# Seven more weights in the one-operand form, and one norm chain in place of two, in a two-block layer of GEMMs on one core

## The chip, the cores and the metric

The kernel runs on one core of a Trainium2 chip: TensorE (PE, the matmuls), VectorE (DVE), ScalarE (ACT), GpSimd (POOL) and SyncE (SP, which issues most transfers). Each engine works through its own instructions in the order in which they were written to it. The metric is the device time of one execution in microseconds, as the median of several runs; less is better.

## The reference

Two blocks work on one sequence of 256 tokens with 2048 features, all in fp32:

```python
# first block
h  = rms_norm(x); u = h @ w_in
y  = concat(ssd_mixer(u[...]), rwkv7_mixer(u[...]))
x1 = x + y @ w_out                                  # w_outa, w_outb
x1 = x1 + memory_cross_attention(rms_norm(x1), mem, wq, wk, wv, wo)
f  = square(relu(rms_norm(x1) @ w1)) @ w2           # w2 as w2a, w2b, w2c
o  = rms_norm(x1 + f, final_norm_g)
# second block
h  = rms_norm(o, attn_norm_g); u = h @ w_in2 + b_in
a  = sliding_window_attention(q, k, v, sinks)       # q, k, v from u
s  = s5_ssm(...)                                    # a diagonal complex recurrence, then gelu and a GLU
x2 = x1 + merge(gates from u, a @ w_ba, s @ w_bs) @ w_out2
x2 = x2 + conv_gated_ffn(rms_norm(x2))              # w_up, w_da, w_db
y  = rms_norm(x2, end_norm_g)
```

The two norms at the seam matter here. With p3 the sum of squares of x over the features and p4 that of x times the final norm's weight, the first is 1/sqrt(p3/D + eps) = c3, the second 1/sqrt(c3^2 p4/D + eps) = c4, and the input of w_in2 is x with both weights times c3 c4.

## The kernel before

Activations lie transposed, 128 features by 256 tokens, and each is kept as hi and lo, two tiles whose sum is the fp32 value. Weights are streamed in units of 128x1024 numbers. For each unit the core gets a transfer (raw), an ACT cast to hi (`wh`) and a DVE subtraction that leaves lo (`wl`). Then TensorE sums wh·hi + wh·lo + wl·hi in PSUM for each K-tile of 128x128 weights. In the narrow form these are three matmuls of 256 columns. In the wide form, which the table `WIDE` (line 29) gives to the first so many blocks of a weight, hi and lo lie side by side and are one operand of 512 columns:

```python
if pair and wide:
    both = acts[c + k].rearrange("p a n -> p (a n)")
    ops = ((pss[n], wh[:, k, s], both), (o, wl[:, k, s], hi))
else:
    ops = ((o, wh[:, k, s], hi), (o, wh[:, k, s], lo), (o, wl[:, k, s], hi))
```

The wide form leaves its sum in two halves of a PSUM bank. At the end of an output's K-tiles, `gemm` folds them: an ACT copy of the second half into a tile `fold...` from the pool `tm` (8 tiles, shared with the rotation tables of the SSM), and a DVE add of the first half. In the narrow form the evacuation reads PSUM itself. Matmuls rotate through 4, 5 or 7 PSUM banks (`NMM, NMB, NMC`), by phase; the second projection runs with five.

Beside the GEMMs run side chains as Python generators (the cross attention, the sliding window attention with its softmax, `ws`, `wsc`, `wp`, `wt`, `wo`, the SSM `s5`, the norms), stepped by a meter that keeps an estimate of each engine's time (tables `FIXED` and `RATE`). A scheduler then sets the order of each engine's instructions from its own estimate of when each could start, so the order on an engine is not that of the code. `s5` works in pairs of channel tiles: `bu` (matmuls), a rotation by the tables `tc` and `tsn` (the tiles r1, r2), a scan (`xi`), the rotation back, `py` (matmuls), gelu. Each of its tables is six GpSimd products of 128x256 in `s5_table` (line 1281). `norm34` (line 1656) makes the two norms at the seam, c3 with `rms_col`, then c4 with `rsqrt_small`, which takes fifteen or so DVE instructions on 128x2 numbers each; `row` turns the result into a row that every evacuation of w_in2 multiplies by (`evac_in2`, line 1684).

In the trace w_in2 goes by the name `w_in` (a number at the end of a name is left out), w1 by `w`, and w_out2, w_outa by `w_out`, `w_outa`. All operations are recorded by one helper, hence L268 throughout.

Of the kernel before, what the change touches and what calls it, by code (L numbers as in the profile page):

```python
# [14 lines left out]
ALU = mybir.AluOpType  # L15
# [3 lines left out]
D = 2048  # L19
EPS = 1e-6  # L20
# [5 lines left out]

NMM, NMB, NMC = 4, 5, 7

WIDE = {"w_in": 8, "w1": 16, "w2a": 4, "w2b": 4, "w2c": 2, "w_out2": 4, "w_up": 22, "w_da": 4, "w_db": 4}


LIVE, OL, LAT, XS = 4, 4, 0.28, 1.0
# [25 lines left out]
def _flat(w, widths):  # L58
# [3 lines left out]
    for width in widths:  # L62
# [7 lines left out]
CUT_D = [512] * 3 + [256, 128, 128]  # L70
# [2 lines left out]
CUT_O = [256] * 8  # L73
SEQ = [("w_in", range(len(CUT_IN))), ("wk", range(len(CUT_K))), ("wv", range(4)), ("w_outa", range(len(CUT_O))), ("w_outb", range(len(CUT_O))), ("wq", range(4)), ("wo", range(4)),
       ("w1", range(6)), ("w2a", range(4)), ("w1", range(6, 11)), ("w2b", range(4)),
       ("w1", range(11, 16)), ("w2c", range(4)), ("w_in2", range(12)), ("w_ba", range(4)),
       ("w_glu", range(2)), ("w_bs", range(4)), ("w_out2", range(4)), ("w_up", range(11)), ("w_da", range(4)),
       ("w_up", range(11, 22)), ("w_db", range(len(CUT_D)))]
WIDTHS = {
    "w_in": CUT_IN,  # L80
    "wk": CUT_K, "wv": [512] * 4, "w_outa": CUT_O, "w_outb": CUT_O, "wq": [512] * 4, "wo": [512] * 4,
    "w1": [512] * 16, "w2a": [512] * 4, "w2b": [512] * 4, "w2c": [512] * 4,
    "w_in2": [512] * 11 + [256],
    "w_glu": [512] * 2, "w_ba": [512] * 4, "w_bs": [512] * 4, "w_out2": [512] * 4,
    "w_up": [512] * 22, "w_da": [512] * 4, "w_db": CUT_D,
# [218 lines left out]
class Net:  # L304
# [54 lines left out]
    def pair(self, pl, name, dt=F32):  # L359
        return pl.tile([P, 2, S], dt, tag="p", name=name)  # L360
# [123 lines left out]
    def gemm(self, name, acts, evac, blocks=None, moving_w=False, hook=None):  # L484
# [5 lines left out]
        for blk in (range(len(widths)) if blocks is None else blocks):  # L490
            width = widths[blk]
            wide = blk < WIDE.get(name, 0)
            base = sum(widths[:blk]) // P
# [787 lines left out]
    def s5_table(self, i):  # L1281

        gp = self.nc.gpsimd
        (cl, sl), (ch, sh) = self.tab
        lo = lambda a: a[:, i].unsqueeze(1).broadcast_to((P, 16, 16))
        hi = lambda a: a[:, i].unsqueeze(2).broadcast_to((P, 16, 16))
        w = lambda a: a.rearrange("p (a b) -> p a b", a=16)
        tmp = lambda n: self.tm(f"{n}{i}")
        c, s, t = self.g(f"tc{i}"), self.g(f"tsn{i}"), tmp("tt")
        self.mul(w(c), hi(ch), lo(cl), gp)  # L1290
        self.mul(w(t), hi(sh), lo(sl), gp)
        self.sub(c, c, t, gp)
        t = tmp("tu")
        self.mul(w(s), hi(sh), lo(cl), gp)
        self.mul(w(t), hi(ch), lo(sl), gp)
        self.add(s, s, t, gp)
        return c, s

    def s5(self):
        nc = self.nc  # L1300
        nxt = self.s5_table(0)
        b2 = lambda a: a.broadcast_to((P, 2, S))
        pair = lambda a: a.rearrange("p (a t) -> p a t", a=2)
        for qd in range(4):
            uh, ul = self.split(self.u2[qd], f"u2s{qd}")
            bh, bl = self.s5b
            y = self.t(f"s5y{qd}")
            for e0 in (0, 2):
                rot = []
                pts = self.pst2(f"bu{4 * qd + e0}")  # L1310
                rows = [slice(32 * e, 32 * e + 32) for e in (e0, e0 + 1)]
                self.beside([(pts[d][:, a * S:(a + 1) * S], b[rows[d], a, qd], u[rows[d]], n == 0, n == 2)
                             for a in range(2) for n, (b, u) in enumerate(((bl, uh), (bh, ul), (bh, uh))) for d in range(2)])
                i0 = 4 * qd + e0
                tabs, turned = [], []
                for d in range(2):
                    w = pair(pts[d])
                    ct, sn = (a.unsqueeze(1) for a in nxt)
                    nxt = self.s5_table(i0 + d + 1) if i0 + d < 15 else None
                    t1, t2 = pair(self.t2(f"r1_{i0 + d}")), pair(self.t2(f"r2_{i0 + d}"))  # L1320
                    self.mul(t1, w, b2(ct))
                    self.mul(t2, w, b2(sn))
                    tabs.append((ct, sn))
                    turned.append((t1, t2))
                yield
                for d in range(2):
                    i = i0 + d
                    (ct, sn), (t1, t2) = tabs[d], turned[d]
                    self.add(t1[:, 0], t1[:, 0], t2[:, 1])
                    self.sub(t1[:, 1], t1[:, 1], t2[:, 0])  # L1330
                    xi = pair(self.t2(f"xi_{i}"))
                    mg = self.s5mag[:, i:i + 1].broadcast_to((P, S))
                    for a in range(2):
                        nc.vector.tensor_tensor_scan(xi[:, a], mg, t1[:, a], 0.0, op0=ALU.mult, op1=ALU.add)
                    self.mul(t1, xi, b2(ct))
                    self.mul(t2, xi, b2(sn))
                    self.sub(t1[:, 0], t1[:, 0], t2[:, 1])
                    self.add(t1[:, 1], t1[:, 1], t2[:, 0])
                    rot.append(t1)
                    yield  # L1340
                py = self.pst(f"py{qd}{e0}")
                self.beside([(py[32 * e:32 * e + 32, :S], cz[:, 4 * qd + e], rot[e - e0][:, a], a == 1, a == 0)
                             for a, cz in ((1, self.czi), (0, self.czr)) for e in (e0 + 1, e0)])
                r = slice(32 * e0, 32 * e0 + 64)
                self.stt(y[r], self.u2[qd][r], self.v("ssm_d", qd)[r], py[r, :S], ALU.mult, ALU.add)
                yield
            self.act(y, y, AF.Gelu)
            self.gl[qd] = self.split(y, f"gl{qd}")
            yield
# [3 lines left out]
def tile_net(ctx, tc, io, out):  # L1353
    m = Net(ctx, tc, io)
    nc = m.nc
    pool = lambda name, bufs: ctx.enter_context(tc.tile_pool(name=name, bufs=bufs))
# [9 lines left out]
    R, C = m.R, m.C  # L1366
# [217 lines left out]
    m.gemm("w_outb", Late(mix, 8), evac_o1)  # L1584
    mix = m.mix = None
    m.banks(NMB, "b")
    m.side(m.norm_rows(acc1, D, EPS, "x"))
    m.qT, m.oT = [None] * 16, [None] * 16

# [42 lines left out]
    xb, acc3, acc4 = [None] * 16, m.g("acc3"), m.g("acc4")  # L1632
# [23 lines left out]
    def norm34():  # L1656
        yield
        yield
        c3 = m.rms_col(acc3, D, EPS, "r3")
        p4 = m.col_sums(acc4, "r4ss")  # L1660
        v4 = m.small("r4v", 2)
        m.mul(v4, c3, c3)
        m.mul(v4, v4, p4[:, 0:2])
        m.ts(v4, v4, 1.0 / D, EPS, ALU.mult, ALU.add)
        c4 = m.rsqrt_small(v4, 2, "r4")
        c34 = m.small("c34", 2)
        m.mul(c34, c3, c4)
        yield
        R["r34"] = m.row(c34, "row34")
        yield  # L1670
        R["r3"] = m.row(c3, "row3")

    m.side(norm34())
    bq8 = m.sp.tile([P, 8], F32, tag="bq8", name="bq8", bufs=1)
    late(m.ts(bq8, m.v("b_q", 0, 8), 0.125, None, ALU.mult))
# [149 lines left out]
```

## Time and profile before

| | |
|---|---|
| median of three runs (lowest, highest) | 2894.16 us (2894.05, 2896.27) |
| profiled execution | 2892.04 us |
| its span, first to last instruction | 2890.1 us |
| mean granted TensorE clock | 0.991 of full speed |
| TensorE, VectorE, ScalarE, GpSimd busy | 98%, 70%, 49%, 10% of the span |
| read from HBM | 497.23 MB, 173 GB/s over the span |

The span and what lies around it (1.9 us) make up the profiled execution, which is 2.1 us below the median. Busy shares are averages over some twenty GEMMs. What matters for a change is the stretch in which it lies: windows and the chain of waits show there who is full and who is waited for.

### The profile page before, as it was taken

What the parts mean: (1) busy time and instruction counts of PE and PEld (TensorE: products, weight loads), DVE (VectorE), ACT (ScalarE), POOL (GpSimd) and SP (SyncE); (2) the same over time, 40 slices, a digit from 0 to 9 for tenths busy, and PEclk for the clock granted to TensorE, in tenths of its full rate; (3) what the DMA queues carried; (4) which work ended last, traced back from release to release, by engine and by line L of the source; (5) the groups of instructions that cost most, each with busy time, mean ns of one, the idle gap of its engine ahead of it and who ended that gap; (6) DMA issues with size and microseconds to landing.
All of it is one profiled execution on the core that took longest, in us unless ns stands there. A gap on an engine that the chain in (4) does not pass through costs nothing.

```text
span 2890.1 us, 50224 instructions
## 1 busy us (share of the span) xinstructions
PE 2836.9 (98%) x19668; PEld 2595.5 (90%) x19668; DVE 2015.4 (70%) x3689; ACT 1422.8 (49%) x2251; POOL 291.3 (10%) x590
## 2 busy tenths in 40 slices
PE   8999999999999999999999899998999999999998
PEld 7999999899999889889889899988988888888887
DVE  7887886577567765565666878877777675577665
ACT  6564643345455544454455445543555454444444
POOL 3333533000000000000000331310000000000000
PEclk9999999999999999999999999999999999999999
DMA  6544444465445665656555544444556555555554
GB/s 218 172 152 130 151 140 141 159 197 182 154 154 183 189 190 184 190 188 193 188 188 178 165 155 160 154 156 138 188 183 192 188 189 187 188 185 188 187 189 145
DMA packets 146253, 502.59 MB, mean 174 GB/s; under 512 B 16352, under 2 KB 25312, under 8 KB 146016
## 3 DMA queue, kind: packets, MB, share of 16 engines
q1 hardware_dynamic: 146016, 499.39, 54.3%
q8 instruction: 154, 2.52, 0.4%
q14 instruction: 83, 0.68, 0.1%
HBM read 497.23 MB, written 2.10 MB: 173 GB/s over the span
## 4 chain that ended last, share of the span: by engine, by line
PE 94%; DVE 2%; POOL 2%; issue 1%; ACT 1%; DMA 0%; SPq 0%; DVEq 0%; ACTq 0%; POOLq 0%
PE mm_w_up L268 17%; PE mm_w_in L268 16%; PE mm_w L268 12%; PE mm_w2a L268 5%; PE mm_w_db L268 4%; PE mm_w_da L268 4%; PE mm_w2c L268 4%; PE mm_w2b L268 4%; PE mm_wk L268 3%; PE mm_wo L268 3%; PE mm_wq L268 3%; PE mm_wv L268 3%; PE mm_w_out L268 3%; PE mm_w_ba L268 2%; PE mm_w_outb L268 2%; PE mm_w_outa L268 2%
## 5 line engine op out<-in xcount | busy, mean ns | idle before, releaser
L268 PE MATMUL mm_w_up<-xu,wh_w_up 128*128 128x512 f32 x1408 | 487.9, 397 | 0.0
L268 PE MATMUL mm_w_up<-xu,wl_w_up 128*128 128x256 f32 x1408 | 376.6, 280 | 0.0
L268 PE MATMUL mm_w<-xf,wh_w 128*128 128x512 f32 x1024 | 350.6, 392 | 0.0
L268 DVE TENSOR_TENSOR wl_w_up<-raw_w_up,wh_w_up 128x1024 fp32r<-128x1024 f32 x176 | 215.4, 1224 | 148.2 <-ACT wh_w_up L268 147.5
L268 PEld LDWEIGHTS mm_w_up<-xu,wh_w_up 128*128 128x128 f32 x1408 | 256.9, 188 | 54.7
L268 ACT CAST wh_w_up<-raw_w_up 128x1024 fp32r<-128x1024 f32 x176 | 184.9, 1050 | 236.0 <-PE mm_w_up L268 220.8
L268 ACT CAST wh_w_in<-raw_w_in 128x1024 fp32r<-128x1024 f32 (+1 forms) x189 | 197.0, 1044 | 195.9 <-PE mm_w_in L268 102.4
L268 PE MATMUL mm_w_in<-ins,wh_w_in 128*128 128x256 f32 (+1 forms) x1248 | 287.2, 315 | 5.9 <-DVE ins L268 5.9
L268 DVE TENSOR_TENSOR wl_w_in<-raw_w_in,wh_w_in 128x1024 fp32r<-128x1024 f32 (+1 forms) x189 | 238.2, 1265 | 69.7 <-ACT wh_w_in L268 69.1
L268 PEld LDWEIGHTS mm_w_up<-xu,wl_w_up 128*128 128x128 f32 x1408 | 265.6, 189 | 9.8
L268 PE MATMUL mm_w<-xf,wl_w 128*128 128x256 f32 x1024 | 273.4, 280 | 0.0
L268 PE MATMUL mm_w_in<-xb,wh_w_in 128*128 128x256 f32 x1472 | 269.9, 285 | 1.2 <-DVE in L268 1.1
L268 DVE TENSOR_TENSOR wl_w<-raw_w,wh_w 128x1024 fp32r<-128x1024 f32 x128 | 156.7, 1225 | 122.0 <-ACT wh_w L268 120.4
L268 PEld LDWEIGHTS mm_w_in<-xb,wh_w_in 128*128 128x128 f32 x1472 | 227.9, 191 | 6.2 <-issue 3.6
L268 PEld LDWEIGHTS mm_w_in<-ins,wh_w_in 128*128 128x128 f32 x1248 | 206.4, 192 | 18.4 <-DVE ins L268 5.9
L268 PEld LDWEIGHTS mm_w<-xf,wh_w 128*128 128x128 f32 x1024 | 186.7, 188 | 35.9
L268 PE MATMUL mm_w_in<-ins,wl_w_in 128*128 128x256 f32 x768 | 213.6, 286 | 3.6 <-DVE wl_w_in L268 3.6
L268 PE MATMUL mm_w_in<-xb,wl_w_in 128*128 128x256 f32 x736 | 206.5, 285 | 2.7 <-DVE wl_w_in L268 2.7
L268 ACT CAST wh_w<-raw_w 128x1024 fp32r<-128x1024 f32 x128 | 134.3, 1049 | 144.2 <-PE mm_w L268 123.0
L268 PEld LDWEIGHTS mm_w<-xf,wl_w 128*128 128x128 f32 x1024 | 192.4, 188 | 7.0
L268 PEld LDWEIGHTS mm_w_in<-ins,wl_w_in 128*128 128x128 f32 x768 | 147.9, 193 | 8.2 <-DVE wl_w_in L268 5.3
L268 PEld LDWEIGHTS mm_w_in<-xb,wl_w_in 128*128 128x128 f32 x736 | 139.1, 191 | 5.8 <-DVE wl_w_in L268 3.1
(1523 smaller groups left out, 7226.4 us busy)
## 6 DMA issues: line engine op xcount, KB each, us to landing
raw_w_in<-in_w_in_dram SPq DMA_DIRECT2D x187, 512.0 KB, 3.6
raw_w_up<-in_w_up_dram SPq DMA_DIRECT2D x176, 512.0 KB, 3.9
raw_w<-in_w_dram SPq DMA_DIRECT2D x128, 512.0 KB, 4.2
raw_w2a<-in_w2a_dram SPq DMA_DIRECT2D x48, 512.0 KB, 4.3
raw_w_da<-in_w_da_dram SPq DMA_DIRECT2D x44, 512.0 KB, 4.0
raw_w_db<-in_w_db_dram SPq DMA_DIRECT2D x42, 512.0 KB, 4.2
raw_w2b<-in_w2b_dram SPq DMA_DIRECT2D x40, 512.0 KB, 3.9
raw_w2c<-in_w2c_dram SPq DMA_DIRECT2D x40, 512.0 KB, 4.3
```

The source lines that it names most:

```text
L268: return f(o, *a, **k)
```

## The change

Four things change. The table `WIDE` gets wk, w_outa, w_outb, wo and w_in2, all their blocks, and takes w2c and w_db whole. w2c's columns are cut like w_db's, 512 three times, then 256, 128, 128. `norm34` sums both squares into one PSUM tile and makes c3 and c3 c4 in one chain on 128x4 numbers: c3 c4 = 1/sqrt(p4/D + eps (p3/D + eps)). And `s5` begins with a GpSimd copy that reads the row of c3 c4, with the table products held in program order behind it; the meter counts GpSimd cheaper from the cross attention on.

```diff
-WIDE = {"w_in": 8, "w1": 16, "w2a": 4, "w2b": 4, "w2c": 2, "w_out2": 4, "w_up": 22, "w_da": 4, "w_db": 4}
+WIDE = {"w_in": 8, "wk": 8, "w_outa": 8, "w_outb": 8, "wo": 4, "w1": 16, "w2a": 4, "w2b": 4, "w2c": 6, "w_in2": 12, "w_out2": 4, "w_up": 22, "w_da": 4, "w_db": 6}
...
-    "w1": [512] * 16, "w2a": [512] * 4, "w2b": [512] * 4, "w2c": [512] * 4,
+    "w1": [512] * 16, "w2a": [512] * 4, "w2b": [512] * 4, "w2c": CUT_D,
...
-        self.mul(w(c), hi(ch), lo(cl), gp)
-        self.mul(w(t), hi(sh), lo(sl), gp)
-        self.sub(c, c, t, gp)
+        pin = self.tc.keep_in_program_order
+        pin(self.mul(w(c), hi(ch), lo(cl), gp))
+        pin(self.mul(w(t), hi(sh), lo(sl), gp))
+        pin(self.sub(c, c, t, gp))
...
     def s5(self):
         nc = self.nc
+
+        nc.gpsimd.tensor_copy(self.small("s5go", 1), self.R["r34"][:, 0:1])
         nxt = self.s5_table(0)
...
+    m.meter.FIXED, m.meter.RATE = dict(m.meter.FIXED, pool=0.1), dict(m.meter.RATE, pool=0.0018)
...
-        c3 = m.rms_col(acc3, D, EPS, "r3")
-        p4 = m.col_sums(acc4, "r4ss")
-        v4 = m.small("r4v", 2)
-        m.mul(v4, c3, c3)
-        m.mul(v4, v4, p4[:, 0:2])
-        m.ts(v4, v4, 1.0 / D, EPS, ALU.mult, ALU.add)
-        c4 = m.rsqrt_small(v4, 2, "r4")
-        c34 = m.small("c34", 2)
-        m.mul(c34, c3, c4)
-        yield
-        R["r34"] = m.row(c34, "row34")
-        yield
-        R["r3"] = m.row(c3, "row3")
+
+        pt = m.pst("r34ss")
+        m.col_sums(acc3, "r3ss", pt[:, 0:2])
+        m.col_sums(acc4, "r4ss", pt[:, 2:4])
+        v = m.small("r34v", 4)
+        m.ts(v[:, 0:2], pt[:, 0:2], 1.0 / D, EPS, ALU.mult, ALU.add)
+        m.ts(v[:, 2:4], v[:, 0:2], EPS, None, ALU.mult)
+        m.stt(v[:, 2:4], pt[:, 2:4], 1.0 / D, v[:, 2:4], ALU.mult, ALU.add)
+        y = m.rsqrt_small(v, 4, "r34")
+        R["r34"] = m.row(y[:, 2:4], "row34")
+        yield
+        R["r3"] = m.row(y[:, 0:2], "row3")
```

Two places show how the order moves. The first is VectorE at the seam. Before, this is the end of the second of two chains (r4), with weight subtractions of w_in2 between:

```order
L268 TENSOR_SCALAR r4v<-r4v 128x2
L268 TENSOR_TENSOR r4t<-r4y 128x2
L268 TENSOR_TENSOR r4t<-r4t,r4v 128x2
L268 SCALAR_TENSOR_TENSOR r4y<-r4t,r4y 128x2
L268 TENSOR_TENSOR wl_w_in_1_2_19391<-raw_w_in_1_2_19328,wh_w_in_1_2_19390 128x1024
L268 TENSOR_TENSOR r4t<-r4y 128x2
L268 TENSOR_TENSOR r4t<-r4t,r4v 128x2
L268 SCALAR_TENSOR_TENSOR r4y<-r4t,r4y 128x2
L268 TENSOR_TENSOR r4t<-r4y 128x2
L268 TENSOR_TENSOR r4t<-r4t,r4v 128x2
L268 SCALAR_TENSOR_TENSOR r4y<-r4t,r4y 128x2
L268 TENSOR_TENSOR c_19260<-r3y,r4y 128x2
```

Now the one chain (r34) stands there:

```order
L268 TENSOR_SCALAR r34v<-r34ss 128x2
L268 TENSOR_SCALAR r34v<-r34v 128x2
L268 SCALAR_TENSOR_TENSOR r34v<-r34ss,r34v 128x2
L268 TENSOR_SCALAR r34t<-r34v 128x4
L268 TENSOR_SCALAR r34y<-r34t 128x4
L268 TENSOR_SCALAR r34v<-r34v 128x4
L268 TENSOR_TENSOR r34t<-r34y 128x4
L268 TENSOR_TENSOR r34t<-r34t,r34v 128x4
L268 SCALAR_TENSOR_TENSOR r34y<-r34t,r34y 128x4
L268 TENSOR_TENSOR wl_w_in_1_0_18630<-raw_w_in_1_0_18578,wh_w_in_1_0_18629 128x1024
L268 TENSOR_TENSOR r34t<-r34y 128x4
```

The chain has 15 instructions in all where there were 29, with one weight subtraction inside it. On GpSimd, in the same place of the program, the first product of a table now stands behind the copy that reads the row:

```order
L268 COPY s5go<-row_18539 128x1
L268 TENSOR_TENSOR tc_18928<-ct_12207,ct_11961 128x256
L268 TENSOR_TENSOR tt_18930<-st_12208,st_11962 128x256
L268 TENSOR_TENSOR tc_18928<-tc_18928,tt_18930 128x256
L268 TENSOR_TENSOR tsn_18929<-st_12208,ct_11961 128x256
L268 TENSOR_TENSOR tu_18934<-ct_12207,st_11962 128x256
```

The second place is VectorE at the start of block 8 of w_in2 (`wl_w_in2_8_c` is the low part of its weight unit at K-tile c, `mm_w_in2_7_n` the sums of block 7, `wsc`, `wmx` and `wsm` belong to the softmax, `r1`, `r2` and `xi` to the SSM). Before, the evacuations of block 7 (sg, from PSUM) lie ahead of the fourth subtraction of block 8:

```order
L268 TENSOR_TENSOR wl_w_in2_8_4_21929<-raw_w_in2_8_4_21834,wh_w_in2_8_4_21928 128x1024
L268 SCALAR_TENSOR_TENSOR wsc60_21509<-cst_98,ws6_21511 128x128
L268 SCALAR_TENSOR_TENSOR wsc61_21510<-cst_98,ws6_21511 128x256
L268 SCALAR_TENSOR_TENSOR wsc60_21509<-cst_98,ws6_21511 128x128
L268 SCALAR_TENSOR_TENSOR wsc61_21510<-cst_98,ws6_21511 128x256
L268 TENSOR_TENSOR sg28_21893<-mm_w_in2_7_0_21585,row34_19400 128x256
L268 TENSOR_TENSOR sg29_21907<-mm_w_in2_7_1_21586,row34_19400 128x256
L268 TENSOR_REDUCE wmx6_21506<-wsc60_21509 128x2
L268 TENSOR_TENSOR sg14_20458<-mm_w_in2_7_2_21587,row34_19400 128x256
L268 TENSOR_REDUCE wmx6_21506<-wsc61_21510 128x2
L268 TENSOR_TENSOR sg15_20467<-mm_w_in2_7_3_21588,row34_19400 128x256
L268 TENSOR_TENSOR wl_w_in2_8_6_22021<-raw_w_in2_8_6_21881,wh_w_in2_8_6_22020 128x1024
```

Now 40 instructions stand between that subtraction and the first fold of block 7, of which these are the last eleven with the fold:

```order
L268 TENSOR_TENSOR wsm7_20691<-wsm7_20691,wes7_20692 128x4
L268 RECIPROCAL wsm7_20691<-wsm7_20691 128x4
L268 TENSOR_TENSOR u2s2l_20772<-in24_18871,u2s2h_20771 128x256
L268 TENSOR_SCALAR wsc70_20693<-wsc70_20693,wsm7_20691 128x128 x2
L268 TENSOR_SCALAR wsc71_20694<-wsc71_20694,wsm7_20691 128x256 x2
L268 TENSOR_TENSOR r1_8_20799<-bu8_20776,tc8_20378 128x512
L268 TENSOR_TENSOR r2_8_20800<-bu8_20776,tsn8_20379 128x512
L268 TENSOR_TENSOR r1_9_20813<-bu8_20776,tc9_20789 128x512
L268 TENSOR_TENSOR r2_9_20814<-bu8_20776,tsn9_20790 128x512
L268 TENSOR_TENSOR r1_8_20799<-r1_8_20799,r2_8_20800 128x256 x2
L268 TENSOR_TENSOR r1_9_20813<-r1_9_20813,r2_9_20814 128x256 x2
L268 TENSOR_TENSOR foldw_in228_20831<-foldw_in228_20831,mm_w_in2_7_0_20541 128x256
```

Rotations of the SSM that stood several blocks later, and the end of a softmax, have moved ahead of the adds that empty the banks of block 7. On ScalarE, the copy that the fold needs stands behind the gelu of the SSM and the softmax's exp and transposed weights (`wt`):

```order
L268 ACT_TABLE_LOAD
L268 ACTIVATE s5y1_19910<-s5y1_19910 128x256
L268 ACT_TABLE_LOAD
L268 ACTIVATE wsc70_20693,wsm7_20691<-wsc70_20693,wmx7_20690 128x128 x2
L268 ACTIVATE gl1h_20738<-s5y1_19910 128x256
L268 ACTIVATE wsc71_20694,wsm7_20691<-wsc71_20694,wmx7_20690 128x256 x2
L268 ACTIVATE wes7_20692<-wes7_20692 128x4
L268 ACTIVATE u2s2h_20771<-in24_18871 128x256
L268 ACTIVATE wt07_20887<-wp07_20879 128x256
L268 ACTIVATE wt17_20888<-wp17_20880 128x512
L268 ACTIVATE foldw_in228_20831<-mm_w_in2_7_0_20541 128x256
```

Before, ScalarE had no part in emptying these banks.

## Rows read from the trace of the kernel before

**Rows 1.** The page, part 1: busy time of each engine, its share, instructions.

```profile
PE 2836.9 (98%) x19668; PEld 2595.5 (90%) x19668; DVE 2015.4 (70%) x3689; ACT 1422.8 (49%) x2251; POOL 291.3 (10%) x590
```

**Rows 2.** The chain of the whole span: start us, us, engine, tile, matmuls.

```profile
649.75 46.09 PE mm_w_outb L268 x384
...
1179.11 111.20 PE mm_w L268 x640
...
1513.53 113.71 PE mm_w2c L268 x832
```

**Rows 3.** Groups by line and shape: busy us, mean ns of one, idle before.

```profile
L268 ACT ACTIVATE foldw_up<-mm_w_up 128x256 f32<-128x256 f32 x88 | 33.6, 382 | 17.8 <-PE mm_w_up L268 17.5
...
L268 DVE TENSOR_TENSOR foldw_up<-foldw_up,mm_w_up 128x256 f32<-128x256 f32 x88 | 32.8, 414 | 0.0
```

**Rows 4.** The chain in 1620 to 1680.

```profile
1641.43 0.41 DVE r3t L268
...
1646.04 0.56 DVE r3t L268
...
1659.83 0.66 DVE c L268
...
1660.62 1.19 PE row34b L268 x4
```

**Rows 5.** Windows at the seam: us, busy (instructions) of each engine, PEclk, DMA, GB/s.

```profile
1645.00:1650.00 5.00, 5.00 (x45) 5.00 (x44) 4.76 (x9) 2.10 (x2) 5.00 (x9) 1.00 0.33 116
1650.00:1655.00 5.00, 1.94 (x15) 1.52 (x13) 4.83 (x10) 0.00 (x0) 5.00 (x8) 1.00 0.33 105
1655.00:1660.00 5.00, 0.00 (x0) 0.00 (x0) 4.79 (x8) 1.04 (x1) 5.00 (x7) 0.59 0.32 105
1660.00:1665.00 5.00, 4.38 (x20) 4.41 (x21) 5.00 (x7) 1.29 (x3) 5.00 (x6) 0.50 0.37 107
1665.00:1670.00 5.00, 5.00 (x41) 5.00 (x40) 3.89 (x11) 1.81 (x5) 2.01 (x4) 0.89 0.31 107
```

**Rows 6.** The tile r6t, then GpSimd's and VectorE's timelines: start us, us, instruction.

```profile
L268 DVE TENSOR_TENSOR r6t<-r6y x3: 161/161/161, 2878.3 to 2879.5; 128x2 f32<-128x2 f32 x3
...
1646.54 0.62 POOL L268 TENSOR_TENSOR tsn<-st,ct 128x256 f32<-128x256 f32 x1
...
1649.65 1.84 DVE L268 TENSOR_TENSOR wl_w_in<-raw_w_in,wh_w_in 128x1024 fp32r<-128x1024 f32 x1
```

**Rows 7.** Windows later in the second projection.

```profile
1900.00:1910.00 10.00, 6.56 (x53) 5.97 (x53) 10.00 (x15) 2.11 (x2) 6.29 (x6) 0.92 0.22 78
1910.00:1920.00 10.00, 10.00 (x66) 8.98 (x63) 10.00 (x19) 4.04 (x6) 0.00 (x0) 0.74 0.35 115
...
2000.00:2010.00 10.00, 5.21 (x36) 3.76 (x34) 7.95 (x15) 1.05 (x1) 0.00 (x0) 0.87 0.42 144
2010.00:2020.00 10.00, 8.46 (x49) 8.44 (x49) 5.81 (x13) 4.99 (x10) 0.20 (x4) 0.62 0.14 52
```

**Rows 8.** Groups of VectorE by shape in 1660 to 2020.

```profile
L268 DVE TENSOR_TENSOR wl_w_in<-raw_w_in,wh_w_in 128x1024 fp32r<-128x1024 f32 x82 | 103.2, 1267 | 23.7 <-ACT wh_w_in L268 23.4
L268 DVE TENSOR_TENSOR r<-r,r 128x256 f32<-128x256 f32 x64 | 26.0, 450 | 0.0
L268 DVE TENSOR_TENSOR_SCAN xi<-mag,r 128x256 f32<-128x256 f32 x32 | 22.0, 720 | 1.1 <-PE wp L268 1.1
...
L268 DVE TENSOR_TENSOR r<-bu,tc 128x512 f32<-128x512 f32 x16 | 10.9, 682 | 1.1 <-PE bu L268 1.1
...
L268 DVE TENSOR_REDUCE wmx<-wsc 128x2 f32<-128x512 f32 x8 | 5.4, 675 | 0.0
```

**Rows 9.** VectorE's timeline: two neighbours.

```profile
1795.85 0.69 DVE L268 TENSOR_TENSOR r<-bu,tc 128x512 f32<-128x512 f32 x1 [0.79 <-PE bu L268]
1796.45 0.68 DVE L268 TENSOR_TENSOR r<-bu,tsn 128x512 f32<-128x512 f32 x1
```

**Rows 10.** Groups of ScalarE in 1660 to 2020.

```profile
L268 ACT ACT_TABLE_LOAD x5 | 6.4, 1283 | 0.1
```

More of the change, by code (lines that the diff above doesn't have):

```diff
@@ L75 @@
        ("w1", range(6)), ("w2a", range(4)), ("w1", range(6, 11)), ("w2b", range(4)),
-       ("w1", range(11, 16)), ("w2c", range(4)), ("w_in2", range(12)), ("w_ba", range(4)),
+       ("w1", range(11, 16)), ("w2c", range(len(CUT_D))), ("w_in2", range(12)), ("w_ba", range(4)),
        ("w_glu", range(2)), ("w_bs", range(4)), ("w_out2", range(4)), ("w_up", range(11)), ("w_da", range(4)),
@@ L1289, in s5_table @@
         c, s, t = self.g(f"tc{i}"), self.g(f"tsn{i}"), tmp("tt")
-        self.mul(w(c), hi(ch), lo(cl), gp)
-        self.mul(w(t), hi(sh), lo(sl), gp)
-        self.sub(c, c, t, gp)
+        pin = self.tc.keep_in_program_order
+        pin(self.mul(w(c), hi(ch), lo(cl), gp))
+        pin(self.mul(w(t), hi(sh), lo(sl), gp))
+        pin(self.sub(c, c, t, gp))
         t = tmp("tu")
-        self.mul(w(s), hi(sh), lo(cl), gp)
-        self.mul(w(t), hi(ch), lo(sl), gp)
-        self.add(s, s, t, gp)
+        pin(self.mul(w(s), hi(sh), lo(cl), gp))
+        pin(self.mul(w(t), hi(ch), lo(sl), gp))
+        pin(self.add(s, s, t, gp))
         return c, s
```

## The prediction

> **What bounds the kernel now.** I read the page first, for who is full: TensorE is busy 98% of the span, VectorE 70%, ScalarE 49% [rows 1]. So every microsecond taken from the matmul stream counts, unless the stream is then starved by somebody. Second, the chain over the whole span, for what one matmul costs: a long unbroken piece there is a stretch in which TensorE waited for nothing, so its length over its count is a price. In w_outb, 384 matmuls take 46.09 us, 0.120 us each; in w1, 640 matmuls take 111.20 us, 0.1738 each [rows 2]. Third, the windows, for the places where TensorE is not full. Three matter, all in the second projection (w_in2 to w_glu). Around 1650 to 1670 only 15, 0, 20 and 41 matmuls fall into four windows of 5 us that hold about 44.5 when full [rows 5]; in 1900 to 1920 there are 53 and 66 where 10 us hold 89, in 2000 to 2020 there are 36 and 49 [rows 7]. Fourth, the chain inside the first of these: a string of tiny VectorE instructions on 128x2 numbers, about 0.56 us each (r3, then r4), ends in c at 1659.83, and only then TensorE moves again, with row34b [rows 4]. The same instruction takes 161 ns in the last norm (r6), where GpSimd has no work; here GpSimd is full with the rotation tables, one 128x256 product after another [rows 6].
>
> **Wide units.** A K-tile of 128x128 costs three 256-column matmuls narrow, 3 x 0.120 = 0.360 us, and one of 512 and one of 256 wide, 2 x 0.1738 = 0.3475 us [rows 2]. Difference 0.0125 us. From the widths and the table, the tiles that turn wide are: wk 256, w_outa 128, w_outb 128, wo 256, w2c 128, w_in2 736, w_db 44; together 1676, and 1676 x 0.0125 = 20.95 us, where TensorE sets the pace. The row of w2c agrees with both prices: 832 matmuls as 128 wide and 192 narrow tiles give 128 x 0.3475 + 192 x 0.360 = 113.6 us against 113.71 [rows 2]. (The Trainium skill, "TensorE: Matmul & The Clock Gate", section Back-to-back issue gap, puts a fixed cost of about 2.5 ns on a warm matmul beside its columns. As an estimate by it a tile saves one such cost, and the sum would be 1676 x 2.5 ns = 4.2 us instead of 20.95. The rows here hold both forms and show five times as much, so the rows decide.)
>
> Each newly wide output needs a fold: an ACT copy of 0.38 us and a DVE add of 0.41 us before its old evacuation [rows 3]. There are about 120, so some 46 us of ACT and 50 us of DVE. In wk, w_outa, w_outb, wo and w2c TensorE is the full engine and VectorE and ScalarE have gaps, so I cost these folds at nothing; if that cover were gone the whole of their time would be on the path, at most 74 x 0.8 = 59 us, which a stage whose VectorE is 70% busy excludes. In the last block of w_db the last fold has no cover: nothing follows but the tail, so +0.38 + 0.41 = +0.8 us.
>
> **The norm.** Twenty-nine small instructions become fifteen, and GpSimd may not start a table before row34 exists, so each of the fifteen should cost what r6's cost, 0.16 to 0.2 us, about 3 us in all with one or two weight subtractions in between. Against that, the old string lasts from 1641.4 to 1660.5. The new order puts TensorE's row34b inside the first block, and the folds empty the PSUM banks of that block without row34, so TensorE has no reason to stand. What it lost: 76 matmuls of 4 x 44.5 = 178 in 1650 to 1670 [rows 5], 102 x 5/44.5 = 11.4 us. That includes the low clock afterwards: granted 0.59 and 0.50, which is TensorE at its lower level of 1.2 GHz [rows 5]. I take -11.2. Bounds: nothing, if row34 is late through other work on VectorE, and -12.
>
> **What the folds do inside w_in2.** Here I leave "hidden". Before, an output of a block is evacuated by one VectorE multiply reading PSUM, and it stands ahead of the block's fourth weight unit. After, the order of VectorE has 40 instructions between that unit (wl_w_in2_8_6) and the first fold of block 7, the add that frees the bank that TensorE's second column group of block 8 needs; the ACT half of it stands behind two table loads, an exp and the wt copies. TensorE can do only the first group (8 tiles, 2.8 us) and the side matmuls (about 4 us). Price of the 40 from rows of the same kinds [rows 8]: one weight subtraction 1.27, eight 128x512 products 8 x 0.68, four scans 4 x 0.72, eight sums 8 x 0.45, and nineteen smaller ones at 0.16 (as r6's) to 0.675 (the softmax's maximum), 6.7 in all; together 19.9 us by durations. Neighbours overlap: a 0.68 instruction is followed after 0.60 [rows 9], so I take off 40 x 0.075 and have 16.9. ACT's hops add about 4 (two table loads of 1.283 [rows 10], gelu, exp). 16.9 + 4 - 2.8 - 4 = 14.1, and 2 more before wl_w_in2_8_8, which stands 19 instructions further on: block 8 loses about 16 us. By the same count block 4 has 29 instructions, 11 us, and 33 us of VectorE work in the block against 24.7 of TensorE: 7 lost. Block 7 has 19, 7 us: 4 lost. Other blocks have 5 or fewer and lose nothing. After each stall the clock has to come back; the stall at 1904 costs (89 - 66) x 0.1125 = 2.6 us that way, at a clock of 0.74 [rows 7]. Two to three of these: 5. Together +32 us. Bounds: 5, if VectorE runs so far ahead that the pile is worked off in its idle time, and 50, if GpSimd's tables, now spread over these blocks, slow the pile as they slowed r3 (a weight subtraction of 1.84 us instead of 1.27 [rows 6, 8]).
>
> (The Trainium skill, "SBUF — State Buffer", section Who interferes with whom, says that a VectorE instruction with two SBUF inputs contends with a GpSimd instruction that reads SBUF, and one with at most one SBUF input outside the two-port modes does not. The trace agrees for the 0.56 against 0.16 of the two-input ones. By it the fold, which reads PSUM and one SBUF tile, is spared, and the products of the s5 pile are not.)
>
> **What goes.** The s5 steps come earlier against the main stream, so the old pile at 1900 to 1910 (53 of 89 matmuls, then 66) [rows 7], (36 + 23) x 0.1125 = 6.6 us, is no longer there in that form; I take -6.5. The wait before w_glu (36 and 49 of 89) [rows 7] lost 10.5 us, of which the s5 tail, now done earlier, was about half: -6. Bounds 0 and -17 for both.
>
> **Sum**, against the profiled execution (2892.04 us; the three runs have their median 2.1 above it): 2892.0 - 20.95 - 11.2 + 0.8 + 32 - 6.5 - 6 = 2880.2 us, so 2882 for the median.
>
> **Rivals.**
> *The pile is harmless.* VectorE is not full in this stage, and in the trace of before it often waits for ScalarE's casts (23.4 us idle before the subtractions [rows 8]), so it may reach the folds earlier than I count. Then new stalls are about 8: 2892 - 44 + 8 + 2 = 2858. Against it: the same counting gives 33.5 us of VectorE work for the old block at 1900, 8 over TensorE's 25.5, and the trace lost 6.5 there.
> *Slower.* One mechanism: in block 8 the chain ws7, softmax, wp7, wt copies, fold goes through three engines, and every hop waits in an in-order queue; if block 8 and block 4 lose twice my price (23 more), and clock recoveries follow, the sum is 2882 + 25 = 2907; half of that gives 2895. It decides from about 44 us of new stalls on (21 + 11.2 + 12.5 - 0.8), where the gain is gone. For it: GpSimd's tables need tiles from the same small pool as the folds, so a late fold can delay a table, and that the next rotation. Against it: no stall of before is over 11.4 us.
> *The norm's wait stays.* If r34 waits on VectorE behind the last w2c folds and the first evacuations, 11 of the gain is gone: 2893, no change.
> *Wide saves nothing here.* If in these seven weights a wide tile costs what a narrow one does, 0.360 us, for instance because its longer operand waits for the next weight load, the 20.95 us stay and the sum is 2903. The rows measure both forms under load; 1 in 100. (The fixed cost of the Trainium skill, above, would make it 2899.)
>
> **Chances.** My sum 0.50, harmless pile 0.23, slower 0.15, norm's wait stays 0.11, wide saves nothing 0.01. A measurement here can tell about 0.2%, 5.8 us. The forecast itself spans 2872 to 2890, so a part of its chance (0.08) falls within 5.8 of 2894.16. Faster 0.42 + 0.23 = 0.65 and a little of the norm case, 0.67; same 0.18; slower 0.15. The range goes from the harmless pile, 2857, to a little over no change, 2896.
>
> **What would show it.** Right: w_outb as 256 matmuls in about 44.5 us without a gap; no small instruction of r34 over 0.25 us and TensorE full in the windows after w2c; idle TensorE of 4 to 18 us at three places about a quarter, a half and two thirds through w_in2, released by VectorE's fold, each followed by a window of clock near 0.7; the last evacuation of w_db 0.8 us later after its matmul. Wrong: w_in2 windows at 85 or more matmul-equivalents throughout (harmless pile), or wide tiles at 0.360 as narrow ones, or a stall at the first block again.

## The result

The change makes the kernel slower: 2918.88 us median (2916.41 to 2920.07) against 2894.11 of before, ratio 1.0085 with a 95% interval of 1.0067 to 1.0102. The prediction was 2882.

The page of the changed kernel says little of it. TensorE is busy for 2 us more than in [rows 1], over a span that is 26.1 us longer:

```profile
PE 2838.9 (97%) x17992; PEld 2512.8 (86%) x17992; DVE 2055.9 (71%) x3796; ACT 1458.1 (50%) x2372; POOL 292.3 (10%) x591
```

So I cut both spans at the first matmul of each GEMM, by its start in the trace, and compare lengths. This table carries the rest of the document.

| from the first matmul of | before, us | after, us | forecast of the step |
|---|---|---|---|
| (start) to wk | 364.4 | 367.6 | 0 |
| wk | 131.0 | 124.2 | -3.2 |
| wv | 106.3 | 111.0 | 0 |
| w_outa | 47.9 | 46.9 | -1.6 |
| w_outb | 46.8 | 53.1 | -1.6 |
| wq | 108.0 | 110.4 | 0 |
| wo | 105.1 | 107.4 | -3.2 |
| w1, w2a, w2b | 603.9 | 608.1 | 0 |
| w2c | 113.7 | 112.9 | -1.6 |
| w_in2 to w_glu | 394.9 | 406.1 | -0.9 |
| w_bs to the end | 868.1 | 868.5 | +0.25 |

Up to w_in2's start 14.5 us are lost where a gain of 11.2 was forecast, and in the second projection 11.2 are lost where a gain of 0.9 was forecast (-9.2 wide, -11.2 norm, -12.5 old waits, +32 new ones). Within the second projection w_in2 itself, up to w_ba, takes 342.6 us instead of 319.4, and w_ba and w_glu together 63.5 instead of 75.5. The tail is as forecast.

**The norm's chain went as planned.** The small instructions of the one chain (the tile r34t; columns as in [rows 6]) cost 161 ns with GpSimd idle, and TensorE is full through the windows where it stood before [rows 5]:

```profile
L268 DVE TENSOR_TENSOR r34t<-r34y x3: 156/161/164, 1656.6 to 1659.3; 128x4 f32<-128x4 f32 x3
```

```profile
1650.00:1660.00 10.00, 10.00 (x62) 8.91 (x61) 6.81 (x21) 3.92 (x4) 0.00 (x0) 1.00 0.60 205
1660.00:1670.00 10.00, 10.00 (x62) 8.88 (x61) 8.12 (x13) 6.05 (x14) 5.01 (x7) 1.00 0.46 154
1670.00:1680.00 10.00, 8.03 (x46) 6.66 (x44) 10.00 (x17) 3.36 (x4) 6.07 (x8) 1.00 0.15 52
```

The third window shows what comes next there: VectorE is full with the sixteen products that scale the residual by the other row, beside the released tables, and TensorE has 46 matmuls where the windows before hold 62.

**Wide itself pays less than its row.** The long pieces of the chain that answer to [rows 2]:

```profile
649.86 45.06 PE mm_w_outb L268 x256
...
1528.83 112.93 PE mm_w2c L268 x704
```

w_outb took 46.09 and takes 45.06: 0.352 us a tile instead of 0.360, a saving of 0.008 where w1's price promised 0.0125. In w2c 128 more tiles turned wide, and the piece went from 113.71 to 112.93: 0.006 a tile.

**At the end of w_outb** TensorE waits for VectorE. Windows, then VectorE's timeline:

```profile
690.00:700.00 10.00, 4.91 (x28) 3.99 (x26) 8.70 (x18) 5.93 (x12) 0.00 (x0) 0.89 0.57 196
700.00:710.00 10.00, 7.22 (x41) 7.22 (x42) 5.52 (x14) 4.18 (x10) 0.00 (x0) 0.60 0.03 14
```

```profile
694.76 2.53 DVE L268 TENSOR_TENSOR wl_wq<-raw_wq,wh_wq 128x1024 fp32r<-128x1024 f32 x2
697.21 0.48 DVE L268 SCALAR_TENSOR_TENSOR xa12l<-xres,vec,xa12h 128x256 fp32r<-128x256 f32 x1
697.61 0.42 DVE L268 TENSOR_TENSOR acc<-acc,sq 128x256 f32<-128x256 f32 x1
697.94 0.41 DVE L268 TENSOR_TENSOR foldw_outb<-foldw_outb,mm_w_outb 128x256 f32<-128x256 f32 x1
698.39 0.42 DVE L268 TENSOR_TENSOR xres<-xin,foldw_outb 128x256 f32<-128x256 f32 x1
```

TensorE has finished w_outb at 694.92. VectorE then still has the low part of output 12 to do, and outputs 13 to 15, each a fold, a residual add, a square's sum and a low part, some 2.2 us apart because ScalarE's high part comes between. wq begins at 702.78, released by the last of these folds after 7.87 us of idle TensorE; the granted clock of that window is 0.60. One window over the whole stretch, before and after, shows why VectorE is late:

```profile
650.00:697.00 47.00, 46.39 (x387) 46.22 (x387) 37.08 (x65) 28.02 (x47) 0.00 (x0) 1.00 0.58 183
```

```profile
650.00:703.00 53.00, 45.13 (x257) 39.03 (x256) 45.41 (x86) 33.73 (x65) 0.00 (x0) 0.95 0.51 179
```

It was busy for 37.08 of 47 us; with sixteen folds of 0.41 more (and some neighbouring work) it needs 45.41, more than the 45.13 for which TensorE is busy. "A stage whose VectorE is 70% busy", as the prediction had it, is an average over the kernel; in this stretch it is 79% before. After, VectorE is not full without a break either: up to 695 it is busy for 38.74 of 45 us, and before the low parts of outputs 13 and 14, for instance, it waits 0.58 us for ScalarE. What is late is a queue of short steps that go back and forth between two engines, and 6.7 us of its VectorE work are left when TensorE has finished.

**In w_in2** the lost windows lie where idle TensorE was forecast, and there are more of them. (Five of the worst; in the 410 us from 1640 the windows of 10 us add up to 32 us of idle TensorE, and to 15 us of work lost to a lower clock, as busy time times what the clock lacks of 1.)

```profile
1740.00:1750.00 10.00, 7.90 (x54) 6.42 (x52) 9.17 (x16) 4.58 (x9) 0.00 (x0) 1.00 0.48 160
1750.00:1760.00 10.00, 6.22 (x33) 3.98 (x34) 9.76 (x28) 2.78 (x11) 0.67 (x1) 0.63 0.00 0
...
1840.00:1850.00 10.00, 5.52 (x41) 3.71 (x41) 9.96 (x24) 2.63 (x11) 1.00 (x1) 0.73 0.32 102
...
1880.00:1890.00 10.00, 2.99 (x22) 1.27 (x20) 8.68 (x22) 2.46 (x5) 0.00 (x0) 0.78 0.16 53
1890.00:1900.00 10.00, 5.18 (x30) 3.77 (x30) 6.25 (x19) 5.91 (x18) 0.00 (x0) 0.50 0.01 2
```

The chain of block 8 goes where it was said to go, from the softmax through the rotations of the SSM to the fold:

```profile
1893.89 1.91 PE bu L268 x10
...
1895.90 3.06 DVE r L268 x6
...
1898.97 0.75 DVE r L268 x2
1899.72 0.33 DVE foldw_in L268
```

But the fold is not what TensorE stands before. These are its largest waits in 1640 to 1960 (what waits, what released it: us in total, times, longest); the complete list has none that a fold released:

```profile
PE mm_w_in L268 <- DVE wl_w_in L268: 8.0, 7, 2.4
...
PE py L268 <- DVE r L268: 6.2, 2, 5.8
...
PE bu L268 <- ACT u2s2h L268: 4.9, 1, 4.9
...
PE bu L268 <- DVE wsc L268: 4.0, 2, 2.8
```

The 5.8 us end at 1887.06 and the 4.9 at 1893.89: block 8's stall lies before `py`, which needs the rotated tiles, and before `bu`, which needs ScalarE's `u2s2h`. w_in2's next matmul comes at 1901.49, right behind a side product, when the first of the folds (done at 1900.05) is already over. The earlier stalls are of the same kind: 2.8 us before `bu` and 2.3 before `ws` around a late `py` from 1748 on, 3.0 before `py` at 1849; two waits of 1.4 at 1784 and 1786 are for weight subtractions. The chain of the first:

```profile
1742.94 1.28 DVE xi L268 x2
...
1751.67 0.68 DVE r L268 x2
...
1752.48 1.92 PE py L268 x8
```

Last, GpSimd's timeline. Between two of its products there is a hole of 47 us, and the product behind it was released by VectorE's read of a folded tile:

```profile
1711.72 0.63 POOL L268 TENSOR_TENSOR tc<-ct,ct 128x256 f32<-128x256 f32 x1
1759.33 1.42 POOL L268 TENSOR_TENSOR tt<-st,st 128x256 f32<-128x256 f32 x1 [46.98 <-DVE in L268]
```

### The profile page after: what moved, and what is told of

It reads as the page before. It is cut to its first block, busy times and chain, and to the rows that moved or that the text cites. A ratio compares the mean times of both kernels' runs of the same rounds, so it can differ in the third digit from the quotient of the medians.

```text
span 2916.2 us, 47104 instructions
## 1 busy us (share of the span) xinstructions
PE 2838.9 (97%) x17992; PEld 2512.8 (86%) x17992; DVE 2055.9 (71%) x3796; ACT 1458.1 (50%) x2372; POOL 292.3 (10%) x591
## 4 chain that ended last, share of the span: by engine, by line
PE 90%; DVE 4%; POOL 2%; ACT 1%; issue 1%; DMA 1%; SPq 0%; DVEq 0%; ACTq 0%; POOLq 0%
PE mm_w_up L268 17%; PE mm_w_in L268 14%; PE mm_w L268 12%; PE mm_w2a L268 5%; PE mm_w_db L268 4%; PE mm_w_da L268 4%; PE mm_w2c L268 4%; PE mm_w2b L268 4%; PE mm_wq L268 3%; PE mm_wv L268 3%; PE mm_w_out L268 3%; PE mm_wo L268 3%; PE mm_wk L268 3%; PE mm_w_ba L268 2%; PE mm_w_outb L268 2%; PE mm_w_outa L268 2%
## 5 line engine op out<-in xcount | busy, mean ns | idle before, releaser
L268 PE MATMUL mm_w_in<-xb,wh_w_in 128*128 128x512 f32 x736 | 263.0, 404 | 0.0
L268 PE MATMUL mm_w_in<-xb,wl_w_in 128*128 128x256 f32 x736 | 199.6, 287 | 8.0 <-DVE wl_w_in L268 8.0
L268 PEld LDWEIGHTS mm_w_in<-xb,wh_w_in 128*128 128x128 f32 x736 | 138.1, 193 | 30.4 <-issue 2.4
```

Source lines behind the costliest of these rows:

```text
L268: return f(o, *a, **k)
```

## The experiments

I began with two theories of the loss in w_in2. A: the folds alone crowd VectorE. B: the tables, held behind the row and put in program order, run at the wrong time. For the loss before w_in2 the rival to the folds was the meter.

**1. w_in2 narrow again.**

```diff
-WIDE = {"w_in": 8, "wk": 8, "w_outa": 8, "w_outb": 8, "wo": 4, "w1": 16, "w2a": 4, "w2b": 4, "w2c": 6, "w_in2": 12, "w_out2": 4, "w_up": 22, "w_da": 4, "w_db": 6}
+WIDE = {"w_in": 8, "wk": 8, "w_outa": 8, "w_outb": 8, "wo": 4, "w1": 16, "w2a": 4, "w2b": 4, "w2c": 6, "w_out2": 4, "w_up": 22, "w_da": 4, "w_db": 6}
```

> The changed kernel with w_in2 in the narrow form again; all else of the change stays. Theory A (the folds of w_in2 put VectorE's SSM and softmax work ahead of the adds that free PSUM banks, and TensorE stands before py and before the second column group): the stage from w_in2 to w_bs falls from 406 us to about 383 (before's 395 less the norm's wait of 11), the piles at 1742, 1838 and 1880 to 1917 are gone, and the kernel takes about 2896; the 15 us lost before w_in2 stay. Theory B (not the folds, but the tables held behind row34 and put in program order make those piles): the stage stays over 400 and the kernel takes 2912 or more.

Measured: 2889.94 us, ratio to before 0.9983 (0.9974 to 0.9993); the stage w_in2 to w_glu takes 379.2 us. The wide form of w_in2, beside the rest of the change, costs 27 us of the 406. B alone falls.

**2. Norm chain, held tables and meter without any wide weight.**

```diff
-WIDE = {"w_in": 8, "wk": 8, "w_outa": 8, "w_outb": 8, "wo": 4, "w1": 16, "w2a": 4, "w2b": 4, "w2c": 6, "w_in2": 12, "w_out2": 4, "w_up": 22, "w_da": 4, "w_db": 6}
+WIDE = {"w_in": 8, "w1": 16, "w2a": 4, "w2b": 4, "w2c": 2, "w_out2": 4, "w_up": 22, "w_da": 4, "w_db": 4}
...
-    "w1": [512] * 16, "w2a": [512] * 4, "w2b": [512] * 4, "w2c": CUT_D,
+    "w1": [512] * 16, "w2a": [512] * 4, "w2b": [512] * 4, "w2c": [512] * 4,
```

> The kernel before with only the one norm chain, the held tables in program order and the cheaper GpSimd in the meter; no weight turns wide. Theory A: the wait of 11 us at the seam goes and no new pile comes, 2882 to 2885. Theory B: the tables now run inside w_in2 and slow VectorE there, 2893 to 2905.

Measured: 2876.86 us, ratio 0.9947 (0.9932 to 0.9962); the stage takes 377.8 us. That is 17.1 less than before, but not where the norm's wait was alone: w_in2 up to w_ba is only 4.3 us shorter, in part because right behind the seam the products with the other row now hold up a weight unit (4.0 us of idle TensorE at 1663, and a granted clock of 0.77 and 0.89 in the windows from 1660 to 1680). The other 12.8 come from w_ba and w_glu, where TensorE no longer waits for the SSM (w_glu takes 14.4 us to w_bs instead of 24.2).

**3. Wide weights without the norm chain, the hold and the meter.** The kernel before with the new `WIDE` and w2c's cut.

> The kernel before with only the wide table and w2c's cut; two norm chains and free tables as before. Theory A: the folds' piles before and in w_in2 are there and the wait at the seam comes back, though the folds let TensorE work on through part of it, 2920 to 2930. Theory B: without held tables the piles of w_in2 are gone, 2880 to 2900.

Measured: 2889.55 us, ratio 0.9989 (0.998 to 0.9999); the stage takes 379.3 us, 15.6 less than before, though it has w_in2 wide and both norm chains, and what comes ahead of it loses as much again (w_in2 begins at 1642.9). Its windows at the seam show no wait at all, with both norm chains in place:

```profile
1650.00:1660.00 10.00, 10.00 (x62) 8.82 (x60) 7.46 (x20) 4.38 (x6) 0.00 (x0) 1.00 0.65 210
1660.00:1670.00 10.00, 10.00 (x61) 8.85 (x60) 7.43 (x25) 4.47 (x7) 0.00 (x0) 1.00 0.50 164
1670.00:1680.00 10.00, 10.00 (x62) 8.91 (x61) 8.13 (x12) 5.76 (x10) 3.77 (x4) 1.00 0.41 124
```

GpSimd, which was full there [rows 5], has nothing to do while the chains run, with no hold (r3's and r4's products take 160 ns), and PSUM banks are freed by folds that need no row; the runs do not part these two. So two edits remove the same wait, and its 11 us can be had once only. Theory A, which gave 2920 to 2930, falls as well, though a part of it stays: TensorE is idle for 12.9 us in 1890 to 1920, before `py` and `bu` as in the changed kernel. Experiments 1 and 2, with w_in2 narrow, lose under 2 us there. Wide alone and norm alone are both not slower; only together do they lose. I formed theory C: the folds and something in the norm part block each other.

**4. The first block's weights narrow.**

```diff
-WIDE = {"w_in": 8, "wk": 8, "w_outa": 8, "w_outb": 8, "wo": 4, "w1": 16, "w2a": 4, "w2b": 4, "w2c": 6, "w_in2": 12, "w_out2": 4, "w_up": 22, "w_da": 4, "w_db": 6}
+WIDE = {"w_in": 8, "w1": 16, "w2a": 4, "w2b": 4, "w2c": 6, "w_in2": 12, "w_out2": 4, "w_up": 22, "w_da": 4, "w_db": 6}
```

> The changed kernel with wk, w_outa, w_outb and wo narrow again; w2c, w_in2 and w_db stay wide. Theory A (the folds of w_outb and wo delay the last residual adds and the next casts, so wq, wo and w1 start late): w1 begins near 910 as before instead of 921, and the kernel takes 2904 to 2908. Rival (the meter's new GpSimd cost, which holds from this phase on, has put the side chains elsewhere): w1 begins at 918 or later and the kernel takes 2917 to 2925.

Measured: 2905.04 us, ratio 1.0043 (1.0028 to 1.0058). w1 begins at 909.8, as before; the meter is out, the folds cause the loss ahead of w_in2. The stage w_in2 to w_glu still takes 405.5 us.

**5. The old meter.**

```diff
-    m.meter.FIXED, m.meter.RATE = dict(m.meter.FIXED, pool=0.1), dict(m.meter.RATE, pool=0.0018)
```

> The changed kernel with the meter's old GpSimd cost; all else stays. So far neither the wide weights alone nor the norm chain with held tables alone loses time, both together do, so theory C: the loss in w_in2 needs the folds and a second cause among the hold, the order of the products and the meter. If it is the meter (side chains stepped at other moments): the w_in2 stage up to w_ba falls from 343 to about 310 and the kernel takes about 2886. If it is the hold: the stage stays at 335 or more, 2910 or more.

Measured: 2911.91 us, ratio 1.0056 (1.0039 to 1.0073). The part up to w_ba takes 326.1 us instead of 342.6, but w_glu waits again (25.0); the whole stage 401.4. Between the two expectations: the meter accounts for 5 of the 28 us by which the changed kernel's stage is longer than experiment 2's.

**6. No hold.**

```diff
-        nc.gpsimd.tensor_copy(self.small("s5go", 1), self.R["r34"][:, 0:1])
```

> The changed kernel without the copy that holds the tables behind row34; the products stay in program order and the meter stays. If the hold is the second cause (the first tables come 20 us later, and all after them): the w_in2 stage up to w_ba is 305 to 315 and the kernel takes about 2886. If it is the meter or the program order of the products: the stage stays at 335 or more, 2910 or more.

Measured: 2918.22 us, ratio 1.0077 (1.006 to 1.0094); stage 406.9. The hold costs nothing.

**7. The tables' temporaries out of the folds' pool.**

```diff
-        tmp = lambda n: self.tm(f"{n}{i}")
+        tmp = lambda n: self.g(f"{n}{i}")
```

> The changed kernel with the tables' temporary tiles taken from the g pool instead of the small pool that the folds use. If the loss comes from that pool (a table waits until a fold's tile has been read, a fold until a table's has, each in program order): GpSimd no longer waits for VectorE's gate multiplies before a table, the w_in2 stage up to w_ba falls from 343 to about 315 and the kernel takes about 2890. If the order of the side chains on VectorE and TensorE is enough by itself: the stage stays at 335 or more, 2910 or more.

Measured: 2899.45 us, ratio 1.0009 (0.9999 to 1.0019). Up to w_ba 301.2 us instead of 342.6, the shortest of all; but w_ba and w_glu take 87.1 together instead of 63.5, as the SSM now ends late; the whole stage 388.3.

**8. Late weights wide, tables free.** The kernel before with the one chain and w2c, w_in2, w_db wide.

> The kernel before with the one norm chain and with w2c, w_in2 and w_db wide, but with tables free, the old meter and the first block's weights narrow. Theory C: no second cause, so the seam's wait is gone or mostly so and no pile comes in w_in2: the stage up to w_ba 300 to 312, 2868 to 2880. If the seam needs the hold (its small instructions slowed by the tables again): 2880 to 2888. If folds in w_in2 with the one chain alone make the piles: 2895 or more.

Measured: 2883.98 us, ratio 0.9962 (0.9947 to 0.9977); stage 385.9. The time lies in the range of the second expectation, but not for its reason: r34's products take 161 ns and TensorE is full through the seam. The stage up to w_ba takes 321.1 us, not 300 to 312, so theory C's claim that no pile comes is missed as well: as in experiment 3, TensorE is idle for 11.7 us at 1890 to 1910, before `py` and `bu`. The stage is 8 us longer than with narrow w_in2 in experiment 2, and no shorter than the 379.3 of experiment 3, which has both norm chains.

**9. Products not in program order.**

```diff
-        pin(self.mul(w(c), hi(ch), lo(cl), gp))
+        self.mul(w(c), hi(ch), lo(cl), gp)
...
```

> The changed kernel without the program order on the tables' products; hold, meter and shared pool stay. If the fixed order is what makes the shared pool costly (a table that waits for a fold's tile holds up all products behind it on GpSimd): the stage from w_in2 to w_bs falls from 406 to 385 or less, and the kernel takes about 2897 or less. If the shared pool is enough with the hold and the meter alone: the stage stays over 398, 2910 or more.

Measured: 2898.55 us, ratio 1.0011 (1.0002 to 1.0021); the stage takes 386.1 us, 20 less than with the order, a little above the first expectation and far from the second. So most of the loss in this stage needs three things together: folds, one pool for folds and tables, and a fixed order on GpSimd. The waits of GpSimd in 1640 to 1960 (waiting tile, releaser: us, times, longest) show it. The changed kernel, then this one, then number 7:

```profile
POOL tt L268 <- DVE sg L268: 78.3, 2, 50.1
POOL tt L268 <- DVE in L268: 65.5, 2, 47.0
```

```profile
POOL tt L268 <- DVE sg L268: 144.0, 7, 41.2
POOL tu L268 <- DVE in L268: 42.1, 2, 41.7
```

```profile
POOL tc L268 <- DVE r L268: 69.4, 3, 55.6
```

A table's second product (`tt`) waits as long for a fold's tile without the order as with it, in all. But without it these waits are many and shorter; with it everything behind the `tt` waits. That tables then come in bursts, and the rotations that use them too, is how I read it; the runs show what the order and the pool cost, not this path step by step. With the temporaries elsewhere no wait for a fold's reader (`sg`, `in`) is left in GpSimd's list.

**10. w_outb narrow.**

```diff
-WIDE = {"w_in": 8, "wk": 8, "w_outa": 8, "w_outb": 8, "wo": 4, "w1": 16, "w2a": 4, "w2b": 4, "w2c": 6, "w_in2": 12, "w_out2": 4, "w_up": 22, "w_da": 4, "w_db": 6}
+WIDE = {"w_in": 8, "wk": 8, "w_outa": 8, "wo": 4, "w1": 16, "w2a": 4, "w2b": 4, "w2c": 6, "w_in2": 12, "w_out2": 4, "w_up": 22, "w_da": 4, "w_db": 6}
```

> The changed kernel with w_outb narrow, all else wide. If the folds of w_outb by themselves make wq late (VectorE's queue of folds, residual adds, squares and low parts is 8 us behind at the end of w_outb): wq begins 47 us after w_outb as before, not 53, and what follows up to w1 loses only wo's own 2 to 3 us, so 6 to 9 us better than the changed kernel, about 2911. Rival (wk's and w_outa's folds have already put VectorE behind): wq still begins 50 us or more after w_outb, and the kernel takes 2916 or more.

Measured: 2906.78 us, ratio 1.0044 (1.0028 to 1.0059). wq begins 46.8 us after w_outb, as before, and takes 108.0: the 6.3 and 2.4 us belong to w_outb's own folds. The time is better than the 2911 expected; 3.4 us of the gain lie before wk, which nothing here changes.

**11. The version that these runs point to.** Norm part as in the change; wide only where VectorE has room.

```diff
-WIDE = {"w_in": 8, "wk": 8, "w_outa": 8, "w_outb": 8, "wo": 4, "w1": 16, "w2a": 4, "w2b": 4, "w2c": 6, "w_in2": 12, "w_out2": 4, "w_up": 22, "w_da": 4, "w_db": 6}
+WIDE = {"w_in": 8, "wk": 8, "w_outa": 8, "w1": 16, "w2a": 4, "w2b": 4, "w2c": 6, "w_out2": 4, "w_up": 22, "w_da": 4, "w_db": 4}
```

> The version that the runs so far point to: one norm chain, held tables and the meter's new cost as in the change, wide only in wk, w_outa, w2c and w_db, whose outputs need little of VectorE; w_outb, wo and w_in2 stay narrow. Theory: 2877 less 1 to 2 (wk with wv behind it), 1 (w_outa) and 1 (w2c): 2872 to 2875. Rival: wk's gain is given back in wv in full, and w2c's folds delay the seam: 2876 to 2880.

Measured: 2872.31 us (2871.78 to 2874.76), ratio 0.9926 (0.9914 to 0.9939): faster than both kernels, some 21 us by the ratio. (The interval overlaps that of experiment 2, so the times alone do not place it ahead of that run.) (The text on record names w_db; in the kernel that ran its last two blocks were left narrow.) wk to w_outb gives 2.0 us against experiment 2 and w2c 1.0. wk is 5.6 us shorter and wv behind it 4.7 longer, so of wk's gain about 1 us is left.

**12. wo alone wide,** beside the norm part.

> The norm chain with held tables as in the run of it alone, and wo alone wide. If wo's folds are covered and the changed kernel lost there only what came late from w_outb: wo and the stretch to w1 take 102 to 103 us (105 narrow), w1 to w2c 603.9, 2873 to 2875. If wo's folds themselves collide with the attention's tail and the norm behind it: wo 106 or more or w1 to w2c 606 or more, 2879 to 2885.

Measured: 2882.76 us, ratio 0.9957 (0.9942 to 0.9972). That is 6 us above experiment 2, 3 by the ratios, whose intervals overlap; the stages show it more clearly. wo takes 110.7 us (106.4 narrow) and the stretch up to w2c 605.5 (603.8). So wo's folds do harm by themselves: wo takes 105.1 to 106.4 us in every run that has it narrow, and 107.0 to 110.7 in every one that has it wide. The chain shows the form of it, which no theory had: late weight buffers, so late transfers, with the norm's and other work (`cells`) on VectorE between them. In experiment 2 the same stretch of the chain is matmuls of wo alone.

```profile
865.25 4.79 DMA raw_wo<-in_wo_dram
870.14 1.06 ACT wh_wo L268
871.23 1.22 DVE wl_wo L268
872.45 0.41 DVE cells L268 x5
...
882.31 5.64 DMA raw_wo<-in_wo_dram
```

Windows that span the second projection but for a us or two close the account. Before; the norm part alone; the changed kernel without program order; the changed kernel:

```profile
1627.00:2022.00 395.00, 373.97 (x3078) 354.69 (x3076) 319.88 (x554) 181.65 (x294) 95.01 (x100) 0.97 0.47 150
```

```profile
1628.00:2006.00 378.00, 365.88 (x3080) 349.60 (x3078) 313.80 (x542) 180.74 (x294) 91.59 (x101) 0.99 0.49 157
```

```profile
1640.00:2024.00 384.00, 363.45 (x2328) 310.02 (x2326) 325.44 (x576) 191.95 (x334) 94.18 (x101) 0.98 0.48 154
```

```profile
1642.00:2048.00 406.00, 373.84 (x2339) 318.07 (x2339) 332.45 (x581) 192.31 (x335) 92.09 (x101) 0.95 0.44 146
```

VectorE is busy for 314 of 378 us with w_in2 narrow. The two windows with it wide hold 12 to 19 us more VectorE work, and wide takes, at 0.008 to 0.0125 a tile, 6 to 9 us from TensorE. In none of the runs with w_in2 wide (379 to 407) is the stage shorter than in experiment 2.

## Why the prediction was wrong

*The wide units.* The step "at 0.0125 where TensorE sets the pace" took w1's price for all. In w_outb a tile saves 0.008. The fixed cost that the Trainium skill gives for a matmul ("TensorE: Matmul & The Clock Gate", Back-to-back issue gap) would make it 0.0025; the measured 0.008, and 0.006 in w2c, lie between the two.

*The step that failed first* is "I cost these folds at nothing", for wk to w2c. It was sized against VectorE's share of the whole kernel. By w_in2's start it is 14.5 against -11.2; 3.2 of the 25.7 between lie before wk and move from kernel to kernel (364.1 to 367.6 over the fourteen profiles). Some 2.5 more are the saving that wk with wv, w_outa and w2c did not bring. Experiments 4, 10 and 12 put the other 20 on the folds of w_outb and wo. The warning was at hand in the trace of before: 37.08 us of VectorE in the w_outb window plus sixteen folds of 0.41 is 43.6 of TensorE's 45, with an evacuation chain behind each.

*The folds inside w_in2.* The places came out near, and the size of the largest too (16 forecast for block 8; the windows from 1880 to 1920 miss 13.9 us of TensorE and some 5 by the clock; 7 and 4 forecast for the others, 5.9 and 4.5 idle in the windows at 1742 and 1838; a third, 2.8 at 1780, was not forecast). The wait was another one. The forecast had TensorE stand before a bank that VectorE's fold frees, with some 4 us of side matmuls to do meanwhile. In the trace no wait of TensorE ends with a fold: it stands before those side matmuls, `py` and `bu`, because the rotations and ScalarE's steps that they need are late. So the pile on VectorE was right and the step from it to TensorE was not, and that the idle time agrees is in part luck. (One aside there is misread as well: of the eight 128x512 products in the pile at least four read `bu` from PSUM, as the fold reads its sum; no term rests on it.) w_in2 up to w_ba, forecast at +5.1 us with all terms, took 23.2 more. What the sum held for a condition of the "slower" rival, that tables and folds share a small pool, was the main thing: with the products in program order it costs 20 us (experiment 9), or 18 by taking the tables out of the pool (experiment 7). I had read in the order that tables follow in order, and in the code that the pool is shared, and gave their meeting 15 in 100.

*The norm* and *what goes* came out smaller and elsewhere. The chain itself is as forecast, 161 ns an instruction and TensorE full beside it. But experiment 2, which has the norm part by itself, is 17.1 us shorter in this stage where the two terms promise 23.7, and 12.8 of these lie in w_ba and w_glu. At the seam the products with the other row, which the sum left out, now hold up a weight unit: 56 matmuls short in 1660 to 1680 in experiment 2 (6 us at 87 in 10 us), 31 short in 1670 to 1690 in the changed kernel (5 us at 62). And experiment 3 loses the wait at the seam by the wide form alone, so the two do not add up as the sum had it. *The tail* was right, +0.4 for +0.25.

Still open: why the stretch up to wk varies by 3 us with nothing of it changed, why wv takes back what wk gains, how a late table becomes a late `py` step by step, and whether a larger shared pool would do as much as experiment 7; none was tried.

## What to carry to other kernels

Price a saving on one engine together with what it puts on another, stretch by stretch: add the new instructions to the busy time of that engine in each stretch's own window, not to its share of the kernel. When two engines draw on one ring of buffers, fixing the order of one of them turns every late reader of the other into a stop for all that stands behind. And two edits that each gain alone can remove the same wait, and block each other besides; run each alone before they are joined.

## What was not expected of the hardware

The stalls cost more than they last. In the windows at and behind them the granted clock was 0.5 to 0.86, which took 15 us of TensorE's work in this stage beside the 32 us of idle time. And a wide tile costs 0.3475 us in w1 and 0.352 in w_outb, with the same two matmuls.
